# Where a decoder trunk's conditioning dots stand in the order, and which pairs VectorE transposes

## The chip, the core and the metric

The kernel runs on one core of a Trainium2 chip. The core has TensorE for matmuls (PE), VectorE (DVE), ScalarE (ACT), GpSimd (POOL) and SyncE (SP), which here only issues DMAs. The metric is the device time of one execution in microseconds (us); the median of several runs is compared.

## What is computed

Two layers of a decoder trunk over 512 positions of 1024 features, all in float32. In each layer a conditioning vector gives shift, scale and gate; the normalised input is projected once into many column groups; three causal mixers work side by side; their gated outputs are projected, weighted and summed, and the sum is projected again and added to the input.

```python
def hybrid_layer(x, c_silu, cos, sin, norm_g, w_ada, b_ada, w_in, sinks, w_br_a, w_br_b, w_br_c, w_out):
    mod = c_silu @ w_ada + b_ada
    shift, scale, gate = jnp.split(mod, 3, axis=-1)
    u = rms_norm(x, norm_g) * (1 + scale[:, None]) + shift[:, None]
    z = u @ w_in
    ...
    ya = dsa_attention(...) * jax.nn.silu(ag)             # A: 128 keys chosen for each query
    yb = swa_sinks_attention(...) * jax.nn.silu(bg)       # B: banded, window 128
    yc = stick_breaking_attention(...) * jax.nn.silu(cg)  # C: strictly causal
    merged = (jax.nn.sigmoid(ma) * (ya @ w_br_a) + jax.nn.sigmoid(mb) * (yb @ w_br_b) + jax.nn.sigmoid(mc) * (yc @ w_br_c))
    return x + gate[:, None] * (merged @ w_out)
```

In mixer C each weight is a sigmoid times a product over the later keys, which the kernel gets from a running sum (a scan) along each row:

```python
    log_beta = jax.nn.log_sigmoid(z)
    log_1m = jnp.where(strict, jax.nn.log_sigmoid(-z), 0.0)
    after = lax.cumsum(log_1m, axis=3, reverse=True) - log_1m
    a = jnp.where(strict, jnp.exp(log_beta + after), 0.0)
```

## The kernel before

**Tiles.** Features lie on the 128 partitions and positions along the free side, so a projection tile is 128 columns by 512 positions. Each float32 operand is split in a high and a low part, and a product is three matmuls (high by high, high by low, low by high). A projection tile (`ttile`) takes two half tiles of 12 matmuls, each fed by one weight chunk of 256 KB. A chunk is loaded into one of four `wstage` slots by SP, and cast and subtracted into `whi` and `wlo` (four slots each) on ACT, DVE or POOL. A branch product (`branch_item`) is one chunk and 12 matmuls, out of the four pairs' outputs y in `Y` (five slots).

**Mixers.** Each has 8 heads, done as 4 pairs. A pair of mixer C goes through `c_qk` (logits into five PSUM banks `ps_s`, the mask, then exponential, logarithm and a scan of each bank), a transpose of the weights, so that the keys lie on the partitions, and a value product (`value_run`), whose output is gated in `finish_pair`. Pairs of A and B do the same with a softmax. The value product of one pair often rides in the same PE group as the low parts of a later pair's logits (`RIDE`): pair 0 of C with the logits of pair 1, 1 with 2, 2 with 3; pair 3 stands by itself.

**Two ways to transpose.** `TR32` lists, for each mixer, the pairs that go by 32x32 blocks: the weights are written into `X` (one slot) in a block order, DVE transposes 32x32 blocks within X in four instructions, and sixteen DMAs, issued on SP and ACT, carry the blocks into `U` (one slot). The other pairs go over PE: twenty transposes of 128x128 (matmuls with the identity, in `small`) into `ps_s`, and five copies into U on ACT or DVE. Pairs 1 and 3 of C and all of A and B go by 32x32 blocks.

**Conditioning dots.** The shift, scale and gate of layer 0's start are made at the beginning. The gate (16 dots a layer) and the shift and scale of layer 1 (32 dots, in layer 0) come from `ada_stream`: each dot loads a chunk of 256 KB into a `wstage` slot, and DVE multiplies it by the conditioning row `csr` and sums. The gate is wanted in the output phase of the same layer, shift and scale at its end.

**The order** is made on the host in two steps. `Weave` merges streams of operations into one list by a clock of its own: an operation moves that clock by its stated cost (`QCOST` for a half tile or a branch product), and a stream that yields `wait(d)` is not asked again until d has passed; `need(e)` holds it until event e is set. The first stream that is free goes next: the dots, the indexer, top-k, mixers C, B and A, and last the projections and branch products, in `by_tile` (`prep_stream` first, `fill_stream` where that is held). `SPACE` has the distances: `c0` ahead of a pair's logits, `c1` between logits and transpose, `c2` between transpose and value product, likewise for a and b; `ag` between gate dots, `as` between shift and scale dots, `t` between top-k steps. Then `Recorder` takes each instruction of that list, models every engine and queue, and puts the instructions in an order of its own by how late each may be. It may run an instruction far from its place in the list, but slots of tiles (`wstage`, `ps_z`, `Y` and so on) are given out in the list's order. What the list holds back by `need` is therefore not a wait on the chip: it is a place in the order.

**What holds what.** The branch products of C need all four pairs of C (event `yc`), and the value products of B beyond pair 0 and those of A need earlier branch products done (`brc`, `brb`), since they take over slots of Y. `bq2`, the queries of B's pair 2, needs B's first transpose (`bfree0`). Mixer A needs top-k and the end of B (`yb`).

Of the kernel before, what the change touches and what calls it, by code (L numbers as in the profile page):

```python
# [39 lines left out]
TOPK = 128  # L40
WARM = 8
BIG = 2.0 ** 100
SPACE = {"c0": 1375, "c1": 7720, "c2": 1666, "a0": 1325, "a1": 18965, "a2": 500, "b0": 2568, "b1": 9198, "b2": 1676, "ag": 12129, "as": 6748, "t": 2422}
QCOST = 2408
BKEY = "cfree2"
LOAD_AHEAD, SPLIT_AHEAD = 4, 3
TR32 = {'a': (0, 1, 2, 3), 'b': (0, 1, 2, 3), 'c': (1, 3)}
RIDE = {('c', 1): (0,), ('c', 2): (1,), ('c', 3): (2,), ('a', 1): (0,), ('a', 3): (1, 2)}
GROUPS = {'c': ((3,),), 'a': ((3,),), 'b': ((0, 1), (2, 3))}

# [581 lines left out]
def op(cost, fn, *chunks):  # L632
    return ("op", cost, fn, [c + (phase[0],) for c in chunks])


def wait(ns):
    return ("wait", ns)


def need(e):  # L640
    return ("need", e)


def put(e):
    return ("set", e)
# [3 lines left out]
def trunk(ctx, tc, xT, vecs, w_ss, w_gt, w_first, w_t, w_v, w_br, w_o, rope, consts, out):  # L649
# [47 lines left out]
    def both(out, a, b, op_):  # L697
        how = ("tensor_tensor", (), dict(out=out, in0=a, in1=b, op=op_))
        rec.add({"DVE": how} if in_psum(a, b) else {"POOL": how, "DVE": how})
# [94 lines left out]
    def ada_ss(l, j, q):  # L794
        return op(0, lambda w: ada_step(l, j, q, w), (w_ss[l, j, q], True))
# [180 lines left out]
    def evac(name, z):  # L976
        kind = name[:2] if name[2:] else name
        if kind in ("ag", "bg", "cg"):
            gate_evac(z, name)
        elif kind in ("ma", "mb", "mc"):  # L980
            m_evac(z, name)
        elif kind == "cq":
            st[name] = stack_q(z, 0.125, sbuf=False)
        elif kind == "ck":
            st[name] = stack_k(z, sbuf=False)
        elif kind in ("aq", "bq", "iq"):
            st[name] = stack_q(rope_evac(z))
        elif kind == "ak":
            st[name] = stack_k(rope_evac(z))
        elif name == "ik":  # L990
            r = key_and_value(z)
            kh, kl = st["ki"] = new_kh(), rec.tile("KI", [P, S], F32R)
            cast(kh[:, 0], r)
            both(kl, r, f(kh[:, 0]), OP.subtract)
        elif name == "bk":
            r = rope_evac(z)
            kh, kl = st["kb"] = new_kh(), new_kh()
            for kv, (a, b) in enumerate(((H0, H1), (H1, H0))):
                cast(kh[a, kv], r[a])
                cast(kh[b, kv], f(kh[a, kv]))  # L1000
                both(kl[a, kv], r[a], f(kh[a, kv]), OP.subtract)
                both(kl[b, kv], r[a], f(kh[a, kv]), OP.subtract)

    def ttile(l, name):
        def half(h):
            def fn(w):
                if h == 0:
                    st["zt", name] = zbank()
                z = st["zt", name]
                hi, lo = w  # L1010
                for i in range(4):
                    k = 4 * h + i
                    wh, wl = hi[:, 128 * i:128 * i + 128], lo[:, 128 * i:128 * i + 128]
                    mm(z, wh, st["uh"][k], k == 0, False)
                    mm(z, wh, st["ul"][k], False, False)
                    mm(z, wl, st["uh"][k], False, k == 7)
                if h == 1:
                    evac(name, st.pop(("zt", name)))
            return op(QCOST, fn, (w_t[l, TIDX[name], h], False))
        return [half(0), half(1)]  # L1020
# [127 lines left out]
    def topk():  # L1148
        yield need("idx")
        for i in (1, 2, 3):  # L1150
            for n in range(TOPK // 8):
# [5 lines left out]
                yield op(0, fn)  # L1157
                yield wait(SPACE["t"])

# [32 lines left out]
    def c_qk(p):  # L1192
        def fn():
# [16 lines left out]
            for bk in (0, 3, 1, 4, 2):  # L1210
# [15 lines left out]
                DVE.tensor_tensor_scan(back, z[:, 1:512][:, ::-1], back, BIG, op0=OP.add, op1=OP.subtract)  # L1226
                if p not in TR32.get("c", ()):
                    ACT.activation(t, t, AF.Exp, scale=-1.0)
# [12 lines left out]
    def mixer_c():  # L1241
        for p in range(4):
            yield need(f"ck{p}")
            yield wait(SPACE["c0"])
            yield from riders("c", p, RIDE.get(("c", p), ()), "in")
            yield c_qk(p)
            yield from riders("c", p, RIDE.get(("c", p), ()), "out")
            yield wait(SPACE["c1"])
            yield softmax_tr("c", p)
            yield put(f"cfree{p}")  # L1250
            yield wait(SPACE["c2"])
            for g in GROUPS["c"]:
# [20 lines left out]
    def softmax_qk(b, p):  # L1273
        def fn():
# [43 lines left out]
            for e in range(2):  # L1318
# [15 lines left out]
                for i in (3, 2, 1, 0):  # L1334
                    bk, c0 = pos(e, i)
                    W = keys(b, i)[1]
                    t = o = pt[bk][:, c0:c0 + W]
                    if p in TR32.get(b, ()):
                        if X is None:
# [19 lines left out]
    def column(b, e, j):  # L1359
        return 7 * e + 2 * j if b == "b" else 4 * j if e == 0 else 16 - 3 * j  # L1360
# [6 lines left out]
    def softmax_tr32(b, p):  # L1367
        def fn():
            pt = st.pop(("p", p))
            pos = bpos if b == "b" else apos  # L1370
            N = blocks(b)
            X = pt
            U = st["V5"][:, :N * P] if p % 2 and b in ('a', 'b') else rec.tile("U", [P, N * P], F32)
            n = N * 32
            for b_ in range(4):
                q = X[:, n * b_:n * b_ + n]
                DVE.transpose(q, q)
                for a_ in range(4):
                    how = ("dma_start", (U[32 * b_:32 * b_ + 32, n * a_:n * a_ + n], X[32 * a_:32 * a_ + 32, n * b_:n * b_ + n]), {})
                    rec.add({"SP": how, "ACT": how})  # L1380
            st["pt", p] = U
        return op(1520 if b == "b" else 2180, fn)

    def softmax_tr(b, p):
        if p in TR32.get(b, ()):
            return softmax_tr32(b, p)

        def fn():
            pt = st.pop(("p", p))
            pos, tpos = (bpos, btpos) if b == "b" else (apos, cpos)  # L1390
            nb = 4 if b == "b" else 5
            tb, PT, left = [None] * nb, [None] * nb, [0] * nb
            for e in range(2):
                for j in range(4):
                    left[tpos(e, j)[0]] += 1
            for e in range(2):
                for j in range(4):
                    bk, c0 = tpos(e, j)
                    if tb[bk] is None:
                        tb[bk] = sbank()  # L1400
                    for i in (range(j, min(4, j + 2)) if b == "b" else range(j, 4)):
                        sbk, s0 = pos(e, i)
                        kc = s0 + 128 * j - keys(b, i)[0]
                        PE.transpose(tb[bk][:, c0 + 128 * (i - j):c0 + 128 * (i - j) + 128], pt[sbk][:, kc:kc + 128], ident)
                    left[bk] -= 1
                    if not left[bk]:
                        W = 384 if b == "b" and bk >= 2 else 512
                        if all(v is None for v in PT):
                            whole = st["V5"] if b != "c" and p % 2 else rec.tile("U", [P, 5 * S], F32)
                        PT[bk] = whole[:, S * bk:S * bk + S]  # L1410
                        cast(PT[bk][:, :W], tb[bk][:, :W])
            st["pt", p] = PT
        return op(1520 if b == "b" else 2180, fn)

    def value_run(b, ps, bank, quads=()):

        quads, ys = list(quads), []
        for p in ps:
# [4 lines left out]
            for j in range(4):  # L1423
                W = min(256, S - 128 * j) if b == "b" else S - 128 * j
                for e in range(2):
# [3 lines left out]
                    o, x = y[64 * e:64 * e + 64, 128 * j:128 * j + W], None  # L1429
                    if p in TR32.get(b, ()):  # L1430
                        lo = column(b, e, j)
# [15 lines left out]
    def riders(b, p, ps, stage):  # L1447
        for q in ps:
            if stage == "out":
                yield put(f"{b}pv{q}")  # L1450
                continue
            yield need(f"{b}g{q}")
            if q and b != "c":
                yield need("brc" if b == "b" else "brb")

    def mixer_ab(b):
# [3 lines left out]
        for p in range(4):  # L1460
            yield need(f"ak{p}" if b == "a" else f"bq{p}")
            yield wait(SPACE[b + "0"])
            yield from riders(b, p, RIDE.get((b, p), ()), "in")
            yield softmax_qk(b, p)
            yield from riders(b, p, RIDE.get((b, p), ()), "out")
            yield wait(SPACE[b + "1"])
            yield softmax_tr(b, p)
# [39 lines left out]
    def branch_item(l, b, d):  # L1507
        def fn(w):
# [16 lines left out]
            if b == "a":  # L1525
# [6 lines left out]
                both(ml, g, f(mh), OP.subtract)  # L1532
        return op(QCOST, fn, (w_br["abc".index(b)][l, d], False))

# [9 lines left out]
        yield put("merged")  # L1544

    def ada_stream(l):
        for j in range(KT):
            for q in range(2):
                yield ada_g(l, j, q)
                yield wait(SPACE["ag"])  # L1550
        if l + 1 < L:
            for j in range(KT):
                for q in range(4):
                    yield ada_ss(l + 1, j, q)
                    yield wait(SPACE["as"])
# [260 lines left out]
```

## Time and profile before

| what | us |
|---|---|
| median of 3 runs | 1126.99 |
| lowest and highest | 1126.3, 1128.29 |
| the profiled execution | 1126.68 |
| its span (first to last instruction) | 1124.6 |

The span holds two layers of about 550 us. In layer 0 the first projections take until 106 us, mixer C runs until about 224, mixer B until 336, mixer A until 472, and branch and output products until about 563. The profile names instructions by what they write and read: `ps_z<-uh,whi` is a matmul of a projection, `ps_z<-Y,whi` of a branch product, `ps_s<-KH,Q` and `klow,Q` logits, `ps_s<-small,t` a transpose on PE, `U,V` a value product, `wstage<-wstage,csr` a dot, `U<-X` a DMA of the block way. All carry line 621 or 619, where the order is written out, so groups are told apart by tiles, not by lines. In the timeline the first two numbers are the start and the length in us; `x20` counts merged instructions; a bracket gives idle time ahead of it and what ended it. In the waits the numbers are the sum in us, the times and the longest. In the stage rows come the stretch, its length, the busy time and count of each engine, the granted clock, the DMA share and GB/s.

### The profile page before, as it was taken

The page shows a single profiled execution, that of the slowest core. Times are in us where ns is not written, and L with a number is a line of the kernel's source. Part 1 is how long each engine was busy: PE and PEld are TensorE (multiplying, and loading weights), DVE is VectorE, ACT ScalarE, POOL GpSimd, SP SyncE. Part 2 cuts the span into 40 slices and gives each one's busy share as a digit, 9 for nine tenths or more (in the row PEclk, how much of TensorE's full clock was granted, in tenths as well). Part 3 has the DMA queues.
Part 4 walks back from the last instruction along what each step waited for, and adds up shares of the span by engine and source line. Part 5 has one row for each costly group of instructions (what it writes and reads, how often), then busy time and mean ns, then how long its engine had stood idle before and what let it go on. Part 6 is the DMA issues. An engine that isn't in the chain of part 4 may idle for free.

```text
span 1124.6 us, 17628 instructions
## 1 busy us (share of the span) xinstructions
PE 1110.1 (99%) x5539; PEld 924.6 (82%) x5539; DVE 922.7 (82%) x2009; ACT 606.3 (54%) x1291; POOL 237.7 (21%) x308
## 2 busy tenths in 40 slices
PE   8999999999999999999999999999999999999997
PEld 6899887788888787788899987777888888877886
DVE  7855999999999898777485389999999979866654
ACT  6744766764546553444355358685446455643343
POOL 1100345420134212010001004561203311211101
PEclk9999999999999999999999999999999999999999
DMA  9744343555365567556544342435635454635343
GB/s 354 237 121 129 94 122 114 141 155 155 111 180 149 171 177 198 150 151 178 173 118 113 103 130 83 136 101 166 180 103 145 137 143 127 180 83 144 94 133 102
DMA packets 95837, 162.48 MB, mean 144 GB/s; under 512 B 15104, under 2 KB 29696, under 8 KB 95744
## 3 DMA queue, kind: packets, MB, share of 16 engines
q1 hardware_dynamic: 86768, 147.60, 45.7%
q10 hardware_dynamic: 8976, 13.77, 4.3%
q8 instruction: 44, 0.72, 0.3%
q14 instruction: 49, 0.40, 0.1%
HBM read 125.39 MB, written 4.19 MB: 115 GB/s over the span
## 4 chain that ended last, share of the span: by engine, by line
PE 89%; DVE 7%; DMA 2%; ACT 1%; issue 1%; SPq 0%; DVEq 0%; ACTq 0%
PE ps_z L621 70%; PE ps_s L621 15%; DVE t L621 3%; PE ps_s L619 3%; DMA U<-X 2%; PE ps_z L619 2%; DMA Y<-in_w_ss 1%; DVE e L621 1%; DVE ps_s L621 1%; DVE wlo L621 0%; DVE KH L621 0%; DVE klow L621 0%; DVE score L621 0%; DVE X L621 0%; SPq L621 0%
## 5 line engine op out<-in xcount | busy, mean ns | idle before, releaser
L621 PE MATMUL ps_z<-uh,whi 128*128 128x512 f32 (+1 forms) x905 | 352.9, 391 | 0.0
L621 PE MATMUL ps_z<-ul,whi 128*128 128x512 f32 (+1 forms) x905 | 351.8, 389 | 0.2 <-DVE ul L621 0.2
L621 PE MATMUL ps_z<-uh,wlo 128*128 128x512 f32 (+1 forms) x905 | 350.8, 388 | 0.0
L621 DVE TENSOR_TENSOR wlo<-wstage,whi 128x512 fp32r<-128x512 f32 (+2 forms) x309 | 205.8, 670 | 89.3 <-ACT whi L621 78.7
L621 ACT CAST whi<-wstage 128x512 fp32r<-128x512 f32 (+2 forms) x232 | 137.1, 593 | 224.7 <-PE ps_z L621 158.3
L621 PEld LDWEIGHTS ps_z<-uh,whi 128*128 128x128 f32 x905 | 169.8, 188 | 35.5 <-issue 1.5
L621 PEld LDWEIGHTS ps_z<-uh,wlo 128*128 128x128 f32 x905 | 169.9, 188 | 34.4 <-issue 0.3
L621 PEld LDWEIGHTS ps_z<-ul,whi 128*128 128x128 f32 x905 | 170.0, 188 | 34.0 <-issue 0.7
L621 POOL CAST whi<-wstage 128x512 fp32r<-128x512 f32 (+1 forms) x74 | 45.8, 619 | 364.3 <-PE ps_z L621 186.8
L621 PE MATMUL ps_z<-Y,whi 128*128 128x512 f32 x384 | 118.9, 390 | 0.5 <-POOL Y L621 0.5
L621 POOL TENSOR_TENSOR wlo<-wstage,whi 128x512 fp32r<-128x512 f32 (+2 forms) x63 | 80.3, 1275 | 160.4 <-DVE whi L621 72.6
L621 ACT ACTIVATE e<-e 128x512 f32<-128x512 f32 x96 | 60.3, 630 | 48.5 <-DVE e L621 35.0
L621 ACT ACTIVATE t<-t,nm 128x256 f32<-128x256 f32 (+3 forms) x128 | 65.3, 512 | 39.1 <-DVE nm L621 17.2
L621 PEld LDWEIGHTS ps_z<-Y,whi 128*128 128x128 f32 x384 | 72.0, 188 | 15.8 <-POOL Y L621 0.8
L621 PE MATMUL ps_z<-Y,wlo 128*128 128x512 f32 x192 | 74.4, 389 | 0.0
L621 ACT ACTIVATE e<-ps_z 128x512 f32<-128x512 f32 x68 | 40.3, 592 | 46.7 <-DMA U<-X 23.6
L621 DVE STREAM_TRANSPOSE X<-X 128x640 f32<-128x640 f32 (+1 forms) x80 | 56.2, 738 | 0.1
L621 ACT ACTIVATE t<-t 128x512 f32<-128x512 f32 x100 | 55.7, 625 | 0.2
L621 DVE MAX8 m<-score 128x8 f32<-128x384 f32 (+2 forms) x96 | 53.2, 556 | 1.4
L621 DVE MATCH_REPLACE8 score<-m,score 128x256 f32<-128x256 f32 (+2 forms) x96 | 52.1, 542 | 0.1
L621 DVE SCALAR_TENSOR_TENSOR wstage<-wstage,csr 128x512 f32<-128x512 f32 x64 | 44.6, 699 | 5.4 <-DMA wstage<-in_w_ss 5.1
L621 PE MATMUL ps_s<-wlo,uh 128*128 128x364 f32 x144 | 47.5, 330 | 0.0
(211 smaller groups left out, 1957.1 us busy)
## 6 DMA issues: line engine op xcount, KB each, us to landing
wstage<-in_w_t SPq DMA_DIRECT2D x212, 256.0 KB, 2.7
wstage<-in_w_v SPq DMA_DIRECT2D x48, 182.0 KB, 2.3
m<-zs SPq DMA_DIRECT2D x128, 64.0 KB, 2.0
wstage<-in_w_gt SPq DMA_DIRECT2D x32, 256.0 KB, 2.7
wstage<-in_w_ss SPq DMA_DIRECT2D x32, 256.0 KB, 2.9
wstage<-in_w_o SPq DMA_DIRECT2D x32, 256.0 KB, 2.7
Y<-in_w_ss SPq DMA_DIRECT2D x15, 512.0 KB, 5.9
U<-X SPq DMA_DIRECT2D x65, 80.0 KB, 3.1
```

The source lines that it names most:

```text
L619: self.real[engine].matmul(*[real(a) for a in q[:3]], start=q[3], stop=True, skip_group_check=True)
L621: made = getattr(self.real[engine], y.op)(*[real(a) for a in y.args], **{k: real(v) for k, v in y.kw.items()})
```

## The change

All three parts are in the same file. The dots' stream is held until event `yb`, the end of mixer B's last value product, in both layers. Pair 2 of mixer C joins pairs 1 and 3 in going by 32x32 blocks. The stated cost of a half tile and five of the distances are set anew: `c0`, `a1`, `b1`, `ag` and `as`.

```diff
-SPACE = {"c0": 1375, "c1": 7720, "c2": 1666, "a0": 1325, "a1": 18965, "a2": 500, "b0": 2568, "b1": 9198, "b2": 1676, "ag": 12129, "as": 6748, "t": 2422}
-QCOST = 2408
+SPACE = {"c0": 864, "c1": 7720, "c2": 1666, "a0": 1325, "a1": 12235, "a2": 500, "b0": 2568, "b1": 703, "b2": 1676, "ag": 2500, "as": 4070, "t": 2422}
+QCOST = 2110
 BKEY = "cfree2"
 LOAD_AHEAD, SPLIT_AHEAD = 4, 3
-TR32 = {'a': (0, 1, 2, 3), 'b': (0, 1, 2, 3), 'c': (1, 3)}
+TR32 = {'a': (0, 1, 2, 3), 'b': (0, 1, 2, 3), 'c': (1, 2, 3)}
...
     def ada_stream(l):
+        yield need('yb')
         for j in range(KT):
             for q in range(2):
                 yield ada_g(l, j, q)
```

## The prediction

> **What bounds the kernel now.** I read the page's busy shares first, then the waits of TensorE (PE), then the busy time by stage, and last the order of time around the work that changes.
>
> ```profile
> PE 1110.1 (99%) x5539; PEld 924.6 (82%) x5539; DVE 922.7 (82%) x2009; ACT 606.3 (54%) x1291; POOL 237.7 (21%) x308
> PE ps_s L621 <- DVE t L621: 2.9, 5, 0.8
> PE ps_s L619 <- DMA U<-X: 1.4, 2, 0.9
> PE ps_z L621 <- POOL Y L621: 0.5, 1, 0.5
> 376.27 27.44 PE ps_z L621 x120
> 106.00:224.00 118.00, 116.16 (x591) 92.78 (x590) 115.25 (x233) 80.88 (x161) 49.03 (x75) 1.00 0.43 115
> 224.00:336.00 112.00, 112.00 (x543) 91.95 (x545) 110.38 (x290) 59.34 (x148) 22.33 (x27) 1.00 0.52 150
> 336.00:525.00 189.00, 189.00 (x883) 153.01 (x880) 161.55 (x365) 96.39 (x204) 37.98 (x35) 1.00 0.60 169
> 886.00:1075.00 189.00, 189.00 (x891) 152.90 (x888) 141.68 (x286) 91.75 (x196) 35.26 (x35) 1.00 0.45 126
> ```
>
> PE is busy for 99% of the span, and its waits sum to a few microseconds. Busy alone proves little, since ends are modelled, so I take the pace: 120 matmuls of 512 columns in 27.44 us are 0.228 us each, and that pace holds wherever the order of time shows no wait. So the time is the sum of PE's work, and an edit can gain only PE work or the few waits. The stage rows (PE, weight loads, VectorE (DVE), ScalarE (ACT), GpSimd, then clock 1.00) show the danger: from 106 to 224 us, where the stick-breaking mixer of layer 0 runs, DVE is busy for 98% (115.25 of 118), in the banded stage for 99%, in the sparse stage for 85% (161.55 of 189) and in that of layer 1 for 75%. The first of these stages is bound twice: by PE, and by one chain of DVE work that feeds PE.
>
> **The transposes that go.** Pair 2 of mixer C is transposed on PE today, 20 blocks in each layer. These rows are of layer 0, then of layer 1.
>
> ```profile
> L621 PE MATMUL ps_s<-small,t 128*128 128x128 f32 x80 | 12.8, 275 | 1.7 <-DVE t L621 1.5
> 181.68 0.39 PE L621 MATMUL ps_z<-uh,whi 128*128 128x512 f32 x1
> 184.02 0.81 PE L621 MATMUL ps_s<-small,t 128*128 128x128 f32 x5 [0.61 <-DVE t L621]
> 189.74 1.20 PE L621 MATMUL ps_s<-KH,Q 128*128 128x512 f32 x7
> ...
> 731.46 0.39 PE L621 MATMUL ps_z<-uh,whi 128*128 128x512 f32 x1
> 733.98 0.77 PE L621 MATMUL ps_s<-small,t 128*128 128x128 f32 x5 [0.61 <-DVE t L621]
> 739.71 0.57 PE L621 MATMUL ps_s<-KH,Q 128*128 128x512 f32 x2
> ```
>
> The 80 transposes are two pairs (0 and 2) in two layers; 40 go. From 181.68 to 189.74 are 8.06 us. They hold the 20 transposes and 20 matmuls of 512 columns, which at 0.228 us take 4.56 us: the transposes cost 3.5 us, 0.7 us of it waits for DVE. In layer 1 it is 739.71 - 731.46 = 8.25 us with the same 20 matmuls: 3.7 us. Together **-7.2 us**. By the group's row alone it would be half of 12.8 + 1.7, also 7.2 us.
>
> [...]
>
> **What takes their place.** Pair 3 goes the new way already, so its rows are the price: eight exponentials into X, four 32x32 transposes on DVE, sixteen DMAs that move the blocks into U.
>
> ```profile
> L621 DVE STREAM_TRANSPOSE X<-X x4: 796/797/832, 209.7 to 211.9; 128x640 f32<-128x640 f32 x4
> L621 ACTq DMA_DIRECT2D U<-X x8: 514/524/608, 210.6 to 216.2; - x8
> L621 SPq DMA_DIRECT2D U<-X x8: 507/507/672, 210.9 to 217.2; - x8
> DMA to landing us min/median/max: 2.0/3.0/3.8
> 219.41 2.37 PE L619 MATMUL ps_s<-U,V 128*64 128x512 f32 x16 [0.90 <-DMA U<-X]
> L621 DVE COPY U<-ps_s x4: 681/683/683, 188.8 to 739.4; 128x512 f32<-128x512 f32 x4
> 187.15 0.61 ACT L621 ACTIVATE t<-t 128x512 f32<-128x512 f32 x1
> 191.77 1.08 PE L619 MATMUL ps_z<-U,V 128*64 128x512 f32 x4
> ```
>
> DVE gains 4 x 0.80 = 3.2 us a layer and loses copies out of PSUM (4 over two layers: 2 x 0.68 = 1.4 us a layer). PE gains nothing: the value products read U as they do for pair 3. The issues are 8 x 0.5 us on SP's queue and as many on ACT's, and weight loads queue behind SP's: 6.3 us pass there from the first U load to the last. What counts is latency. From the first transpose of pair 3 (209.7) to the start of its value product (219.41) are 9.7 us, the last 0.9 of it PE waiting. Pair 2's last exponential ends at 187.15 + 0.61 = 187.8; its U would be there at 187.8 + 9.7 = 197.5, where PE starts the value product today at 191.77. That product rides in the same group as the low parts of pair 3's logits, so pair 3's whole chain starts **5.7 us later in each layer**. I cost this at little because PE has other work to do meanwhile, which the slower rival below denies.
>
> **The dots.** Each is a load of 256 KB into one of the four stage slots that the weights share, and a DVE pass.
>
> ```profile
> 106.00:224.00 118.00, 5.54 (x16) 0.00 (x0) 1.00 0.43 115
> 224.00:336.00 112.00, 7.23 (x18) 0.00 (x0) 1.00 0.52 150
> 336.00:525.00 189.00, 19.96 (x58) 0.00 (x0) 1.00 0.60 169
> 503.74 9.43 SPq L621 DMA_DIRECT2D wstage<-in_w_ss  x7
> 513.76 5.27 SPq L621 DMA_DIRECT2D wstage<-in_w_o  x5
> wstage<-in_w_o SPq DMA_DIRECT2D x32, 256.0 KB, 2.7
> L621 ACT CAST whi<-wstage 128x512 fp32r<-128x512 f32 (+2 forms) x232 | 137.1, 593 | 224.7 <-PE ps_z L621 158.3
> L621 DVE TENSOR_TENSOR wlo<-wstage,whi 128x512 fp32r<-128x512 f32 (+2 forms) x309 | 205.8, 670 | 89.3 <-ACT whi L621 78.7
> 521.43 0.39 PE L621 MATMUL ps_z<-V,whi 128*128 128x512 f32 x1
> ```
>
> The first three rows are the same stages, with the DVE time of the instructions on the conditioning row alone (two a dot). So the edit takes 5.5 us off DVE in the C stage and 7.2 us in the B stage of layer 0 and puts 12.8 us into the A stage: DVE there goes from 161.6 to 174.3 of 189 us, 92%, less than the 98% that stages B and C bear today without holding PE. In layer 1 it would be about 154 of 189. I cost both at nothing; PE's splits have POOL and ACT as the other way. Off the cover: if the A stage saturates, each dot costs PE at most its own 0.7 us.
>
> The end of layer 0 is the other place. The old spacing left 7 dots to load after the last branch weights (503.74, 9.43 us, 1.35 us each), and the output weights came behind them. The new: in the planner's time a half tile is 2.11, so distances of 2.5 and 4.07 both mean a dot every second half tile. After the banded mixer I count some 70 half tiles and 9 mixer operations, which place 40 of the 48: 7 to 10 left over, as today. From the first output load (513.76) to its first matmul (521.43) are 7.7 us; a load (2.7 to landing) and its split (0.59 + 0.67) need 4.0. The 3.7 us between cover 2 dots more, so 10 left over would cost 1 dot, 1.35 us, and 9 nothing; I take nothing.
>
> **The distances.** They move no work and take none away; they set who stands ahead of whom in the list from which slots are given. The one that matters is b1, 9198 to 703: bq2, which waits for the first banded transpose, is now listed ahead of the branch products, and can fill PE while the C chain is late. QCOST, c0, a1: between nothing and the size of the waits that PE has today (2.9 + 1.4 + 0.5 us), either way; I take nothing.
>
> **The sum.** -7.2 us of transposes, +1.4 us for a wait on pair 2's U in both layers (pair 3 has 1.4 in its two today), 0 for the rest: -5.8 us. The profiled execution took 1126.68 us (its span is 1124.6); 1126.68 - 5.8 = 1120.9. The median shown, 1126.99, is 0.3 above it: **1121.2 us**. With no new wait it would be 1126.99 - 7.2 = 1119.8, and with today's waits for U and Y gone as well (1.4 + 0.5) 1117.9: there is nothing below that.
>
> **Rivals.**
>
> ```profile
> 198.75 9.01 DVE t L621 x11
> 210.59 3.52 DMA U<-X
> 217.21 1.97 DMA U<-X
> 221.79 2.02 PE ps_s L621 x16
> L621 PE MATMUL ps_z<-Y,whi 128*128 128x512 f32 x12 | 3.5, 390 | 0.0
> ```
>
> First, **the chain of mixer C becomes the bound** (slower). The chain that ended last runs, around 200 us, through DVE's scans and the U transfers, not through PE; and in the 25 us ahead of 219.41 PE already does partial branch products (the row of 12, and 6 more), which is what it does when little else is free. If nothing more can be drawn forward, both layers end 5.7 us later: 1126.7 + 11.4 = 1138. PE has 5.7 + 3.6 = 9.3 us to fill a layer. Drawing the banded logits of pair 1 forward (2.02 us) leaves 7.3, less 3.6 gained: +3.7 a layer, 1134. One projection tile instead (24 x 0.228 = 5.5 us) leaves 3.8: 1127. Tile and logits leave 1.8: 1123. Two tiles and the logits (13 us) cover it. It decides from one tile on: less makes it slower. For it: PE is out of work at 219.41 today. Against it: bq2 comes early, three ps_z banks, and 5.5 us less DVE work.
>
> [...]
>
> Second, **the dots pile up**: 14 left at the end of layer 0 are 7 x 1.35 - 3.7 = 5.8 us of empty PE, and 1127: the gain is eaten. Only a miscount by some five or more does it.
>
> Third, **the dots don't move**: the wait is one of the planner, no semaphore, and its priorities can run a dot as early as slots allow. But slots are given in the listed order, so most must move; time as forecast.
>
> **Chances.** Forecast, with tile and logits drawn or more: 0.60 (1117.5 to 1124). Chain with one tile: 0.13, 1127. Chain with less: 0.17, 1132 to 1138. Dots pile up: 0.10, half near 1127, half above 1129. A measurement of this kernel tells 0.2%, 2.3 us, from no change. So faster 0.60, same 0.18, slower 0.22. The range is 1117 to 1133: it takes in the forecast, the even cases and the cheaper half of the slow ones.
>
> **What would show it.** 40 transposes on ps_s in place of 80, 88 DVE transposes where there were 80; PE waits for U ahead of pair 2's value product under 1 us; pair 3's first mask some 6 us later against qk of pair 2, yet PE busy till then with projections. Wrong: a new PE wait of several us on U, Y or on a stage load between 190 and 230 us or around 515.

## The result and the profile after

The changed kernel takes **1133.41 us** (median of 4 runs, 1132.95 to 1133.99) against 1126.7 for the kernel before on the same chip (1126.3 to 1128.29): a ratio of 1.0057, interval 1.004 to 1.0075. It is slower by about 6.7 us, where 1121.2 was forecast, and just above the range, which ended at 1133. The span of its profiled execution is 1132.1 us, 7.5 more than before.

First the page of the changed kernel: the busy row (engine, busy us, share of the span, instructions), the shares of the chain that ended last, and the group of DVE transposes.

```profile
PE 1107.9 (98%) x5499; PEld 919.1 (81%) x5499; DVE 927.2 (82%) x2021; ACT 605.8 (54%) x1294; POOL 235.1 (21%) x297
...
PE 73%; DVE 16%; DMA 3%; ACT 3%; issue 3%; SPq 1%; POOL 0%; ACTq 0%; DVEq 0%; POOLq 0%
...
L621 DVE STREAM_TRANSPOSE X<-X 128x640 f32<-128x640 f32 (+1 forms) x88 | 61.7, 744 | 2.6 <-ACT X L621 1.6 <-DMA m<-zs 0.9
```

The change is there: 40 PE instructions fewer (5499 against 5539) and 88 DVE transposes. PE is busy for 2.2 us less than before (1110.1), but span less busy time, which is PE's idle time, went from 14.5 us to 24.2. So **2.2 us of busy time were won and 9.7 us of idle time were added**: 7.5, the whole difference of the spans. The same view of the kernel before has PE at 89% of the chain and DVE at 7%:

```profile
PE 89%; DVE 7%; DMA 2%; ACT 1%; issue 1%; SPq 0%; DVEq 0%; ACTq 0%
```

Where the idle time lies, in the changed kernel's busy time by stage (stretch, length, then busy us and count of PE, weight loads, DVE, ACT, GpSimd, then the granted clock, the DMA share and GB/s):

```profile
106.00:224.00 118.00, 112.56 (x551) 89.87 (x549) 112.04 (x213) 73.60 (x144) 51.54 (x74) 1.00 0.38 107
224.00:336.00 112.00, 111.03 (x544) 90.64 (x546) 108.15 (x283) 60.04 (x157) 24.15 (x28) 1.00 0.47 135
336.00:525.00 189.00, 186.82 (x874) 150.24 (x871) 163.92 (x390) 98.26 (x208) 27.58 (x27) 1.00 0.62 182
```

In mixer C of layer 0 PE idles 5.4 us (118 - 112.56) where it idled 1.8, and in the next two stages, which had no idle time at all, 1.0 and 2.2. DVE is less busy in mixer C than before, 112.04 against 115.25, so PE's waits there don't come from more work on DVE.

The waits of PE in the changed kernel (sum, times, longest):

```profile
PE ps_z L619 <- DMA U<-X: 4.8, 3, 2.8
PE ps_s L621 <- DVE t L621: 3.7, 5, 1.3
PE ps_s L621 <- DVE Q L621: 1.6, 2, 1.1
PE ps_s L621 <- ACT KH L621: 1.4, 1, 1.4
PE ps_z L621 <- DVE wlo L621: 1.1, 1, 1.1
```

And its order of time on PE at the value products of C's pairs 1, 2 and 3 and at the first output product of layer 0:

```profile
172.82 1.40 PE L619 MATMUL ps_z<-U,V 128*64 128x512 f32 x6 [2.80 <-DMA U<-X]
...
197.51 2.37 PE L619 MATMUL ps_z<-U,V 128*64 128x512 f32 x16 [1.20 <-DMA U<-X]
...
225.21 2.37 PE L619 MATMUL ps_s<-U,V 128*64 128x512 f32 x16 [0.21 <-issue]
...
527.26 0.39 PE L621 MATMUL ps_z<-V,whi 128*128 128x512 f32 x1
```

Pair 2 starts at 197.51, as worked out (197.5), and pair 3 follows 5.8 us later than before (219.41). The first output product is 5.8 us later too (521.43 before): what layer 0 has lost by pair 3 of mixer C it has still lost at its end. Layer 1 adds 1.7 us. The longest wait, 2.80 us, is not at pair 2 but at **pair 1, which went the block way before as well**. PE is ready for it at 170.02 (before, it started at 171.04), and U comes later. SyncE's queue is shown first for the changed kernel, then for the one before:

```profile
161.25 9.75 SPq L621 DMA_DIRECT2D U<-X  x9
```

```profile
160.87 6.85 SPq L621 DMA_DIRECT2D U<-X  x9
```

Nine issues take 9.75 us in place of 6.85. The group of these issues over the whole changed kernel (count, then ns at least, in the median and at most) has the one that does most of it, 2.23 us, at 166.87:

```profile
L621 SPq DMA_DIRECT2D U<-X x118: 507/580/2228, 161.2 to 984.7; - x118
```

The order around these issues is a new one, although nothing in the change touches pair 1. That is a first sign that the parts of the change are not what it costs.

### The profile page after: what moved, and what is told of

Same layout as the page of the kernel before. It is cut to its first block, busy times and chain, and to the rows that moved or that the text cites. A ratio compares the mean times of both kernels' runs of the same rounds, so it can differ in the third digit from the quotient of the medians.

```text
span 1132.1 us, 17634 instructions
## 1 busy us (share of the span) xinstructions
PE 1107.9 (98%) x5499; PEld 919.1 (81%) x5499; DVE 927.2 (82%) x2021; ACT 605.8 (54%) x1294; POOL 235.1 (21%) x297
## 4 chain that ended last, share of the span: by engine, by line
PE 73%; DVE 16%; DMA 3%; ACT 3%; issue 3%; SPq 1%; POOL 0%; ACTq 0%; DVEq 0%; POOLq 0%
PE ps_z L621 55%; PE ps_s L621 14%; DVE t L621 4%; DVE wlo L621 2%; PE ps_s L619 2%; PE ps_z L619 2%; DVE X L621 2%; DMA m<-zs 2%; SPq L621 1%; DVE zc L621 1%; DVE m L621 1%; DVE wstage L621 1%; DMA U<-X 1%; ACT t L621 1%; ACT KH L621 1%
## 5 line engine op out<-in xcount | busy, mean ns | idle before, releaser
L621 DVE TENSOR_TENSOR wlo<-wstage,whi 128x512 fp32r<-128x512 f32 (+2 forms) x300 | 197.6, 662 | 95.0 <-ACT whi L621 84.5
L621 POOL TENSOR_TENSOR wlo<-wstage,whi 128x512 fp32r<-128x512 f32 (+2 forms) x72 | 91.9, 1279 | 169.8 <-DVE whi L621 71.2
L621 POOL CAST whi<-wstage 128x512 fp32r<-128x512 f32 (+1 forms) x68 | 41.4, 609 | 320.4 <-PE ps_z L621 121.1
L621 ACT ACTIVATE t<-t,nm 128x256 f32<-128x256 f32 (+3 forms) x128 | 65.2, 511 | 32.6 <-DVE nm L621 20.1
L621 DVE STREAM_TRANSPOSE X<-X 128x640 f32<-128x640 f32 (+1 forms) x88 | 61.7, 744 | 2.6 <-ACT X L621 1.6
L621 PE MATMUL ps_s<-KH,Q 128*128 128x256 f32 (+3 forms) x280 | 50.6, 305 | 4.6 <-DVE Q L621 1.6
L621 DVE MAX8 m<-score 128x8 f32<-128x256 f32 (+2 forms) x96 | 53.2, 556 | 1.8
L621 PEld LDWEIGHTS ps_s<-KH,Q 128*128 128x128 f32 x280 | 43.2, 189 | 12.8 <-ACT KH L621 3.1
L621 DVE MATCH_REPLACE8 score<-m,score 128x384 f32<-128x384 f32 (+2 forms) x96 | 52.0, 542 | 0.0
L621 ACT ACTIVATE e<-ps_z 128x512 f32<-128x512 f32 x68 | 40.2, 593 | 20.1 <-DMA V<-X 7.1
```

Source lines behind the costliest of these rows:

```text
L621: made = getattr(self.real[engine], y.op)(*[real(a) for a in y.args], **{k: real(v) for k, v in y.kw.items()})
```

## The experiments

Three theories were to be told apart. **The later U** (the first rival of the prediction): the block way gives pair 2's weights later, and mixer C hangs on that. **The dots** (the second rival): their loads pile up at the end of layer 0. **The order as a whole**: every edit makes the planner set all 17,600 instructions anew, and a new order has more waits on PE than the one before, whatever the edit. Later expectations also call these the chain theory, the dots theory and the scatter or order theory, or name theories by letters of their own. Each ratio is against runs of the kernel before on the same chip; the idle time is span less PE's busy time. The spans are of one execution each, and not all of one chip: the kernel before took 1126.7 to 1128.3 us (medians) on the chips used, so a microsecond or two between spans tells nothing.

| run | median us | ratio, interval | span | PE busy | PE idle |
|---|---|---|---|---|---|
| before | 1126.7 | | 1124.6 | 1110.1 | 14.5 |
| changed | 1133.41 | 1.0057, 1.004 to 1.0075 | 1132.1 | 1107.9 | 24.2 |
| T_alone | 1137.88 | 1.009, 1.0075 to 1.0105 | 1136.1 | 1112.0 | 24.1 |
| D_alone | 1139.01 | 1.01, 1.008 to 1.012 | 1136.6 | 1113.3 | 23.3 |
| S_alone | 1136.33 | 1.0073, 1.0056 to 1.0089 | 1134.6 | 1112.9 | 21.7 |
| DS_no_T | 1132.43 | 1.0041, 1.0026 to 1.0056 | 1130.1 | 1111.8 | 18.3 |
| nudge_2400 | 1133.12 | 1.0048, 1.0033 to 1.0063 | 1130.4 | 1111.9 | 18.5 |
| nudge_2430 | 1147.53 | 1.0172, 1.0145 to 1.0199 | 1141.6 | 1116.9 | 24.7 |
| after_2200 | 1136.16 | 1.0074, 1.0054 to 1.0094 | 1134.0 | 1110.7 | 23.3 |
| after_split | 1136.28 | 1.0079, 1.0057 to 1.0101 | 1134.2 | 1108.4 | 25.8 |
| kept_T | 1147.61 | 1.0186, 1.0169 to 1.0203 | 1145.4 | 1109.1 | 36.3 |
| kept_T_late | 1144.9 | 1.016, 1.0145 to 1.0175 | 1143.0 | 1111.9 | 31.1 |
| kept_T_clear | 1138.18 | 1.0092, 1.0078 to 1.0105 | 1136.2 | 1112.3 | 23.9 |
| kept_T_free | 1132.61 | 1.0044, 1.003 to 1.0057 | 1131.0 | 1110.9 | 20.1 |

### One part of the change at a time

T_alone has only the third pair by blocks, D_alone only the dots' wait with their two distances, S_alone only the stated cost and the other distances; DS_no_T is the changed kernel with pair 2 back on PE.

```diff
-TR32 = {'a': (0, 1, 2, 3), 'b': (0, 1, 2, 3), 'c': (1, 3)}
+TR32 = {'a': (0, 1, 2, 3), 'b': (0, 1, 2, 3), 'c': (1, 2, 3)}
```

> The kernel before with the block transposes of pair 2 of mixer C alone; dots and distances as before. Chain theory (the longer way of pair 2 delays pair 3's chain by 5 to 6 us a layer and PE has nothing to fill it with): 1130 to 1137 us, value product of pair 3 about 6 us later in each layer, waits for U or its successors of several us. Dots theory and distances theory (the loss lies in one of those): 1119 to 1123, the gain of 40 transposes less a small wait. Scatter theory (each new order differs by a few us for no single reason): anything from 1122 to 1132.

```diff
+        yield need('yb')
...
-SPACE = {... "ag": 12129, "as": 6748, ...}
+SPACE = {... "ag": 2500, "as": 4070, ...}
```

> The kernel before with the dots alone moved (held until the end of mixer B, with their two new distances). Chain theory: within 2 us of before (1125 to 1129). Dots theory (their loads crowd the stage slots after mixer B, or pile up at the end of layer 0): 1132 or more, with PE waits on splits after 336 us or around 515 us. Distances theory: as before.

```diff
-SPACE = {"c0": 1375, ... "a1": 18965, ... "b1": 9198, ...}
-QCOST = 2408
+SPACE = {"c0": 864, ... "a1": 12235, ... "b1": 703, ...}
+QCOST = 2110
```

> The kernel before with c0, a1, b1 and the cost of a half tile alone set anew; the dots keep their old places and distances. Chain theory: within 2 us of before. Distances theory: 1131 or more, with PE waits in mixer A of layer 0 where logits or transposes stand elsewhere in the order. Dots theory: as before.

```diff
-TR32 = {'a': (0, 1, 2, 3), 'b': (0, 1, 2, 3), 'c': (1, 2, 3)}
+TR32 = {'a': (0, 1, 2, 3), 'b': (0, 1, 2, 3), 'c': (1, 3)}
```

> The changed kernel with pair 2 of mixer C back on TensorE; dots and distances as changed. Chain theory: 1122 to 1128, the loss is gone, since only the transposes lengthen the chain. Dots or distances theory: 1133 or more, since the loss stays and the gain of the 40 transposes goes. Scatter theory: 1124 to 1132.

Each part alone loses **more than all three together**: 0.9%, 1.0% and 0.73% against 0.57%. The parts don't add up, so no one of them is the cause. Each came out near what the theory of its own part had asked for in time (1130 to 1137 us for T_alone, 1132 and 1131 or more for D_alone and S_alone), but three theories that each claim a loss of 8 to 11 us cannot all hold in a kernel that lost 6.7. And the time alone does not bear them out: none of PE's listed waits in D_alone is for a weight split, and none lies around 515 us, where its theory looked for them.

Without the transposes' part the loss is 0.41%; with it 0.57%, and the two intervals overlap. In spans, that part took 3.9 us off PE's busy time there (1111.8 to 1107.9) and put 5.9 us on its idle time (18.3 to 24.2). PE in DS_no_T, at pair 3's value product and at the first output product of layer 0:

```profile
222.87 2.37 PE L619 MATMUL ps_s<-U,V 128*64 128x512 f32 x16
...
525.51 0.39 PE L621 MATMUL ps_z<-V,whi 128*128 128x512 f32 x1
```

With pair 2 on PE these are 3.5 and 4.1 us later than before (219.41 and 521.43), where the changed kernel has 5.8 and 5.8. So **most of the delay in mixer C is there without the later U**, which can have added about 2 us in layer 0.

S_alone shows the second rival's mechanism, in a kernel that keeps the dots' old distances while a half tile counts for less. Its queue on SyncE, and PE at the first output product:

```profile
504.50 19.61 SPq L621 DMA_DIRECT2D wstage<-in_w_ss  x15
524.40 5.05 SPq L621 DMA_DIRECT2D wstage<-in_w_o  x5
```

```profile
527.66 0.79 PE L621 MATMUL ps_z<-V,whi 128*128 128x512 f32 x1 [5.31 <-ACT whi L621]
```

Fifteen dots are left over, the output weights wait behind them, and PE waits 5.31 us. The changed kernel has no such wait. There the same queue reads

```profile
512.79 9.60 SPq L621 DMA_DIRECT2D wstage<-in_w_ss  x8
522.68 0.94 SPq L621 DMA_DIRECT2D wstage<-in_w_o  x2
```

with 8 dots, and the row of 527.26 above has no bracket. So the dots at the end of layer 0 are not where the changed kernel lost its time.

### The same program in a neighbouring order

These runs change nothing but the planner's stated cost of a half tile, which moves no work and adds none: two around the kernel before, one on the changed kernel.

```diff
-QCOST = 2408
+QCOST = 2400
```

> The kernel before with the stated cost of a half tile 2400 in place of 2408, and nothing else: same instructions, same tiles, another order. Scatter theory (the order before is a lucky one among many, and any edit falls back among the others): 1130 to 1138 us. Any theory that puts the loss on a part of the change (chain, dots, distances): within 1 us of before.

```diff
-QCOST = 2408
+QCOST = 2430
```

> The kernel before with the stated cost of a half tile 2430 in place of 2408: a second neighbour. Scatter theory: 1130 to 1138 us, and not the same as with 2400. Any theory of a part: within 1 us of before.

```diff
-QCOST = 2110
+QCOST = 2200
```

> The changed kernel with the stated cost of a half tile 2200 in place of 2110: the same parts, another order. Scatter theory: differs from the changed kernel by several us, either way (1128 to 1142). Theories of a part: within 1 us of the changed kernel (1133 to 1135).

A step of 0.3% in that number costs 0.48%, one of 0.9% costs 1.72%, with the same 5539 PE instructions. nudge_2430 is above the 1130 to 1138 us that the scatter theory gave it, and its profiled execution is the fastest of its four (1143.41), so the span and idle time in its row are low ones. after_2200 lost 0.74% where the changed kernel lost 0.57%; the intervals overlap. This is the finding that decides: **the kernel before stands in an order that is better than its neighbours**. Of the ten orders that the planner made here it has the least idle time on PE, 14.5 us; the others have 18.3 to 25.8. In nudge_2400, the nearest, no wait stands out. The largest sums are

```profile
PE ps_s L621 <- DVE t L621: 4.0, 6, 0.8
PE ps_z L621 <- DVE G L621: 2.4, 2, 1.2
PE ps_s L621 <- DVE epst L621: 1.0, 1, 1.0
PE ps_z L621 <- POOL Y L621: 1.0, 2, 0.5
PE ps_s L621 <- POOL t L621: 0.8, 2, 0.4
```

The first of them was 2.9 us in the kernel before, the second is not in its list, and the rest is 1.0 us or less each. PE's busy time is 1.8 us up, which is lost pace and not work.

The slower orders were also granted less of PE's clock. Its mean over the profiled execution was 0.993 in T_alone, 0.995 in S_alone and after_2200, 0.996 in D_alone and nudge_2430, and 0.997 in after_split. In the three fastest of the nine it was 0.999 (DS_no_T) and 0.998 (nudge_2400 and the changed kernel), and in the kernel before 0.998 too: so the clock is not what the changed kernel lost. Why the one order is so good was not found out.

### The block way alone, in the order of before

To see the price of the later U without a new order, the last five runs set it apart. after_split leaves the order to the planner, and lets pair 2's value product no longer ride with the low parts of pair 3's logits, but follow them:

```diff
-RIDE = {('c', 1): (0,), ('c', 2): (1,), ('c', 3): (2,), ('a', 1): (0,), ('a', 3): (1, 2)}
+RIDE = {('c', 1): (0,), ('c', 2): (1,), ('a', 1): (0,), ('a', 3): (1, 2)}
+LONE = (2,)
...
+            if p - 1 in LONE:
+                yield from riders("c", p, (p - 1,), "in")
+                yield op(2200, lambda p=p: value_run("c", (p - 1,), zbank))
+                yield from riders("c", p, (p - 1,), "out")
```

> The changed kernel with the value product of pair 2 of mixer C taken out of the PE group of pair 3's low logit parts and put behind it as a group of its own, so that pair 3's chain no longer waits for pair 2's U. Chain theory: pair 3's first mask comes 8 to 13 us earlier against pair 2's logits, the value product of pair 3 at least 4 us earlier, and the time falls to 1122 to 1130. Dots or distances theory: within 2 us of the changed kernel. Scatter theory: 1128 to 1140, without regard to how early pair 3 ends.

It loses 0.79%. Pair 3's value product (this kernel's lines are numbered one higher) starts

```profile
221.66 0.65 PE L620 MATMUL ps_s<-U,V 128*64 128x512 f32 x2 [0.60 <-DMA U<-X]
```

3.6 us sooner than in the changed kernel, a little less than the 4 us that the chain theory asked for. The first output product still comes 2.5 us later than there (529.76 against 527.26), and the time is 1136.28 where that theory had 1122 to 1130. So in a new order a shorter chain of mixer C won nothing back. But it is once more a new order, with 25.8 us of idle time, and the price of the place itself can't be read from it. The other four therefore take the order from a table, the one of the kernel before, instruction for instruction on every engine; pair 2's transposes and copies are replaced by four DVE transposes and sixteen DMAs a layer as soon as its weights are there.

```diff
-TR32 = {'a': (0, 1, 2, 3), 'b': (0, 1, 2, 3), 'c': (1, 3)}
+TR32 = {'a': (0, 1, 2, 3), 'b': (0, 1, 2, 3), 'c': (1, 2, 3)}
...
-        best = None
-        for n in range(self.ROUNDS):
...
-        return best[1]
+        raw, n = zlib.decompress(base64.b85decode(PIN)), len(self.list)
+        perm = np.cumsum(np.frombuffer(raw[:2 * n], np.int16).astype(np.int64)).tolist()
...
+        return [(self.list[i], ("PE", "ACT", "DVE", "POOL", "SP")[raw[2 * n + i]]) for i in perm]
```

> The order of the kernel before kept instruction for instruction on every engine, and only pair 2 of mixer C changed to the block way: its 40 TensorE transposes and 10 copies gone, 12 and 4 more exponentials and DVE transposes and 32 DMAs put in where they can first run; the value product of pair 2 stays where it stood on TensorE, in one group with pair 3's low logit parts. Chain theory: TensorE waits 3 to 6 us for U there in each layer, pair 3 ends 5 to 6 us later and nothing is drawn forward: 1134 to 1140 us. Order theory (the change lost a favourable order, and the longer way of pair 2 matters little): 1120 to 1126 us.

In kept_T the value product stays in its place. Its time is above what either theory had given it (1120 to 1126 and 1134 to 1140 us). The order of time on PE in layer 0, and the waits:

```profile
184.67 0.50 PE L621 MATMUL ps_z<-uh,whi 128*128 128x512 f32 x1 [2.09 <-DVE zc L621]
...
199.73 4.44 PE L619 MATMUL ps_z<-U,V 128*64 128x512 f32 x16 [8.98 <-DMA U<-X]
```

```profile
PE ps_z L619 <- DMA U<-X: 18.5, 2, 9.6
PE ps_z L621 <- DVE zc L621: 4.4, 2, 2.3
```

Here the later U is naked: 18.5 us of waits in two layers, and 20.8 us on the span. The first row holds a second price. In the kernel before, that matmul, the first of a new tile, came behind the transposes:

```profile
184.02 0.81 PE L621 MATMUL ps_s<-small,t 128*128 128x128 f32 x5 [0.61 <-DVE t L621]
184.60 0.50 PE L621 MATMUL ps_z<-uh,whi 128*128 128x512 f32 x1
```

It started at 184.60; without the transposes it starts at 184.67. PE came to it 2.09 us sooner, and then **waited 2.09 us for its PSUM bank**, which DVE empties (`zc`) no sooner than before. The ten transposes ahead of it cost nothing where they stood. At the value product PE arrives at 199.73 - 8.98 = 190.75, where it was at 191.77 before: of the 3.5 us that this layer's transposes were put at, 1.0 was won.

kept_T_late makes the value product a group of its own and puts it later, by what the expectation puts at 5 us of PE work; the trace has eight matmuls more ahead of it than in kept_T, 1.8 us.

```diff
-GROUPS = {'c': ((3,),), 'a': ((3,),), 'b': ((0, 1), (2, 3))}
+LONE = (('c', 3),); GROUPS = {'c': ((3,),), 'a': ((3,),), 'b': ((0, 1), (2, 3))}
...
-        value_run(b, RIDE.get((b, p), ()), zbank, quads)
+        for ps, qs in (((), quads), (RIDE[b, p], ())) if (b, p) in LONE else ((RIDE.get((b, p), ()), quads),):
+            value_run(b, ps, zbank, qs)
```

> As kept_T, but the value product of pair 2 is a group of its own, 5 us (some 22 matmuls of projections) further on in TensorE's order, so that pair 3's logits don't wait for pair 2's U; everything else keeps its place. Chain theory and order theory both: the 40 transposes (4.3 us of work) and their waits go and nothing new is late: 1118 to 1123 us, the waits of TensorE at or below those of before. If it stays at 1126 or more, the DMAs' and DVE's extra work costs by itself (queues, ports), and both theories fall.

```profile
200.41 4.26 PE L619 MATMUL ps_z<-U,V 128*64 128x512 f32 x16 [7.24 <-DMA m<-zs]
```

```profile
189.36 3.59 SPq L621 DMA_DIRECT2D U<-X  x5
193.96 0.33 SPq L621 DMA_DIRECT2D wstage<-in_w_t  x1
194.57 0.33 SPq L621 DMA_DIRECT2D wstage<-in_w_br_c  x1
194.96 1.87 SPq L621 DMA_DIRECT2D U<-X  x3
```

The wait is still 7.24 us, and 1118 to 1123 us had been expected: moving the product moved the wait. The row names another DMA, but what the product reads is U, whose last three loads stand on SyncE's queue behind two weight loads of 256 KB; the product starts at 200.41, where the rows of pair 3 had let expect 197.5.

kept_T_clear changes the table alone: the value product stands 62 matmuls, some 14 us of PE work, later than in kept_T.

> The order of before is kept on every engine, pair 2 of mixer C goes by blocks, and its value product is a group of its own placed one projection tile and a half (some 15 us of TensorE work) later than in before, where its U should long have landed; in the run with 5 us it still waited 7.2 and 5.7 us. Theory A (the price of the block way is the late U alone, with the half clock that the wait brings): the waits ahead of pair 2's value product go (under 0.5 us each), the clock stays full, the 4.3 us of transposes show, less up to 4 us of waits for the rotated values in mixer C's logits that PE now reaches sooner: 1122 to 1127 us. Theory B (the block way costs DVE time and queue time that PE feels elsewhere, whatever the place of the value product): no wait on U of pair 2, but other waits of 5 us and more, at pair 3's value product or at weights, and 1130 to 1140 us. Rival C (the kept order is so tight that any displaced group breaks it): waits on ps_z or Y and over 1135 us.

The wait for pair 2's U is gone; only 0.2 us is left at pair 3's. In its place come the banks, at pair 2's value product too, which was the sign of rival C (the time, 1138.18 us, lies in B's range as well):

```profile
PE ps_z L619 <- DVE zc L621: 6.8, 2, 3.4
PE ps_z L621 <- DVE zc L621: 4.5, 2, 2.3
```

and a thing that had not been looked for, the granted clock. The busy time of kept_T_clear around the first waits, of 2.27 us up to 184.30 and of 3.43 us up to 209.69; the clock stands behind GpSimd's count:

```profile
184.00:188.00 4.00, 3.70 (x10) 2.93 (x11) 4.00 (x9) 2.35 (x6) 0.59 (x2) 0.62 0.55 160
200.00:206.00 6.00, 6.00 (x28) 4.87 (x26) 6.00 (x8) 5.90 (x13) 5.38 (x8) 1.00 0.38 112
206.00:214.00 8.00, 4.57 (x18) 1.72 (x16) 4.35 (x6) 4.28 (x10) 3.84 (x7) 0.68 0.26 66
214.00:218.00 4.00, 4.00 (x22) 3.31 (x19) 3.72 (x6) 1.77 (x3) 0.33 (x2) 0.79 0.29 82
```

After each of these waits PE runs at little more than half its pace for some microseconds and then at full pace again. Ahead of the first its matmuls of 512 columns start 0.23 us apart, from 185.24 to 187.80 0.43 us, and the clock from 200 to 206 is 1.00. Behind the second the sixteen of the value product take 4.54 us, which took 2.37 in the changed kernel, and from 215.87 on the distance is 0.23 again. These waits are paid for twice.

kept_T_free changes the table again: another, empty, bank for the tiles where PE waited, the value product 19 matmuls later still, and the rotation of the tile ahead of it two scans sooner on DVE.

> As kept_T_clear, with the waits that run showed taken away: the projections from the one where TensorE waited 2.27 us (at 184 and 740 us) on are given another of the three banks of ps_z, which stands empty now, the value product of pair 2 stands some 17 matmuls later still, and the rotation of the tile whose bank it takes goes ahead of two scans on VectorE. TensorE now saves its transposes and waits for no bank and for no U of pair 2. Theory A (late U, banks and the half clock after them are the whole price of the block way): no wait of over 1.5 us in mixer C, full clock, 1121 to 1125 us. Theory B (mixer C hangs on its chain through VectorE, so PE that is ahead waits for pair 3 instead): waits of 2 to 4 us a layer ahead of pair 3's value product or of the first branch products that need its Y, and 1125 to 1131 us. Over 1135 us with no such wait would speak against both.

```profile
PE ps_z L621 <- POOL t L621: 2.5, 2, 1.2
PE ps_s L621 <- DVE t L621: 2.3, 5, 0.8
PE ps_s L621 <- POOL Q L621: 1.9, 2, 1.0
PE ps_z L621 <- POOL Y L621: 1.3, 2, 0.7
PE ps_z L621 <- DVE wlo L621: 1.2, 2, 0.6
PE ps_s L619 <- DMA U<-X: 1.2, 2, 0.7
```

Now there is no wait of over 1.3 us left, and the kernel is 15.0 us faster than kept_T, yet still 0.44% slower than before. It came out above the 1125 to 1131 us of the theory of the chain (B). The two waits that this theory named, at pair 3's value product and at the first branch products that need its Y, are there, but with 0.7 us at most in place of 2 to 4. The rest are for splits of weights, rotated queries and logits. All are pieces of work that others do for PE and that are not sooner for PE's being ahead. Pair 3 shows the chain all the same. On PE and on DVE:

```profile
221.74 2.38 PE L619 MATMUL ps_s<-U,V 128*64 128x512 f32 x16 [0.72 <-DMA U<-X]
...
213.78 0.69 DVE L621 TENSOR_TENSOR e<-ps_z,G 128x512 f32<-128x512 f32 x1 [0.88 <-PE ps_z L619]
214.39 0.83 DVE L621 STREAM_TRANSPOSE X<-X 128x640 f32<-128x640 f32 x1
```

Its value product starts 2.3 us later than before (219.41), because its last transpose stands on DVE behind the gating of the displaced pair 2. The four spans from kept_T on, 1145.4, 1143.0, 1136.2 and 1131.0, are one account: PE's idle time falls from 36.3 to 20.1 us as one named wait after the other goes, and what is left is still 5.6 us more than before, more than the 4.3 us that the transposes hold PE (worked out below). No order was found in which the block way of pair 2 pays.

## Why the prediction was wrong

**What bounds the kernel** was read rightly: PE, with an idle time of 14.5 us in all. The chain mattered more than its share of 7% let expect.

**The transposes, -7.2 us.** Too large. Back to back, from one start to the next, they lie 0.109 us apart (median over the trace of before), so 40 hold PE for 4.3 us; the rest of the 7.2 was waiting between them, which need not go with them. And even the 4.3 are only worth something where PE has other work that is ready: in kept_T 1.0 us of a layer's share reached the value product.

**The later U, +1.4 us.** The time was right to the tenth (197.51), but by luck: pair 2's last exponential ended at 188.9 in the new order, 1.1 us later than before, and from the first DVE transpose to the value product took 8.6 us and not 9.7. The wait at pair 2 is 1.20 us in layer 0 and none in layer 1, near the 1.4 forecast. What it sets off was missed: in the order of before it costs 18.5 us of waits. The sign of being wrong that the prediction named, a wait of several microseconds between 190 and 230 us or around 515, did not come; the longest, 2.80 us, came at 172.82.

**The dots, 0.** Right in this kernel: 8 left over where 7 to 10 were counted, no wait at 527.26, DVE far from full in the A stage (163.92 of 189, below the 174.3 expected).

**The distances, 0, or the waits that PE has today (2.9 + 1.4 + 0.5 us) either way.** This is the step that failed. The prediction took the idle time of before as a property of the kernel, which new distances could move by 4.8 us at most. It is a property of one order. The changed kernel has 9.7 us more of it, and S_alone, which has the new cost and distances (but for the dots' own) and nothing else, lost 8.1 us against the kernel before on its chip, with the one wait of 5.31 us among them. All nine other orders that the planner made have 3.8 to 11.3 us more of it, even the one that differs only by 0.3% in a stated cost. With 4.3 us of work taken off and 3.8 to 11.3 us of idle time put on, as is known only now, the forecast would have lain from 0.5 us below the time before to 7.0 above it, and not 5.8 below it.

**The rivals.** The first, the chain of mixer C, has the right place: pair 3 is 5.8 us later and the output phase of layer 0 starts 5.8 us later, as if nothing had been drawn forward. kept_T and its successors show that the mechanism is real and how large it can be. But it isn't the cause by itself: DS_no_T, where pair 2's U is not late, has lost 5.5 of the 7.5 us of span already, 3.5 of it by pair 3; and after_split mends the chain and wins nothing. The second, the dots, didn't come here, though S_alone shows it at 5.31 us. The case that cost the time, a new order that is worse all over, was not among the rivals. How the 7.5 us divide between the parts has no answer, as the parts don't add: by way of DS_no_T the transposes cost 2.0 us, by way of T_alone 11.5 (9.6 by the medians on its chip).

## What to carry to other kernels

Where an order was made by a planner for a kernel that is 99% busy, move a stated cost by a fraction of a per cent and time that first: the spread (here 0.5 and 1.7% for two steps) is what any edit may have to pay for a new order, and an edit that saves less can be lost in it. Work taken off the bounding engine counts only where its next work is ready; look for the wait that comes last right behind it (the bank that another engine empties), which the removed work had been hiding. To price one edit by itself, hold the rest of the order fixed.

## What the runs showed of the hardware

**After some short waits the clock was lower.** In the four kept_T runs the trace grants PE a lower clock for some microseconds after waits of PE: 0.67 from 200 to 206 us in kept_T, 0.81 from 739 to 748 in kept_T_late, 0.62 and 0.68 in the rows of kept_T_clear above, 0.79 from 206 to 214 in kept_T_free. The mean over the profiled execution was 0.990 in kept_T and kept_T_clear, 0.991 in kept_T_late and 0.995 in kept_T_free. In the kernel before the clock was 1.00 from 20 to 1118 us, in the changed one from 20 to 1125. The value product of pair 2 took 4.44 us in kept_T where its sixteen matmuls took 2.37 in the changed kernel.

A single wait isn't the measure: after 2.27 us in kept_T_clear the clock was 0.62 (184 to 188), while around the 2.80 us at 172.82 in the changed kernel it was 1.00 (166 to 182), and in kept_T_free no wait was over 1.3 us, though three of them, 1.21, 0.96 and 0.17 us, lie close together where its clock drops. In kept_T_late the wait for the bank comes once in each layer, 4.5 us in all and 2.3 at most: in layer 1 PE idles 2.26 of the 9 us whose clock was 0.81, and in layer 0 the matmuls that follow, from 185.83 on, start 0.23 us apart, at full pace. What decides was not shown.

**Small transfers take their time.** In the kernel before, a load of U of 80 KB issued on SyncE's queue landed after 3.1 us (median), a weight chunk of 256 KB after 2.7. The same nine issues on that queue took 6.85 us in one order and 9.75 in the other, and the value product that reads the last loads of U in kept_T_late, issued there by 196.83, started at 200.41. That the weight loads ahead of them on that queue held them up is not shown: the last three loads of U on ScalarE's queue, where no weight load stands, were issued from 194.06 to 195.92, and which of these loads came last is not known.
